# Holding VectorE's background work (block differences, weight sums, third modulation vector) at its place in the text's order

## The chip, the cores and the metric

The kernel runs on one core of a Trainium2 chip. A core has TensorE (PE, with its weight loads listed as PEld), VectorE (DVE), ScalarE (ACT), GpSimd (POOL) and SyncE (SP, which here only issues DMAs); each works through an instruction stream of its own, and they meet at semaphores. The metric is the device time of one execution in microseconds, as the median of several runs. The profile is one further execution, recorded by the hardware profiler.

## The reference

One decoder layer over a sequence of 1024 tokens of width 1024. A conditioning vector gives shift, scale and gate; the normalised, modulated input goes through one wide projection; two gated linear recurrences (HGRN2 with 8 heads, GLA with 4) run on parts of it; both results are projected, merged under sigmoid gates, projected once more, multiplied by the gate vector and added to the input.

```python
c_act = jax.nn.silu(c)
mod = c_act @ ada_w[l] + ada_b[l]
shift, scale, gate = jnp.split(mod, 3, axis=-1)
h = rms_norm(x, norm_w[l]) * (1.0 + scale[:, None, :]) + shift[:, None, :]
proj = h @ w_in[l]
hq, hf, hi, hz, gq, gk, gv, gz, ga, mg = jnp.split(proj, IN_OFFSETS, axis=-1)
y_h = hgrn2_branch(hq, hf, hi, hz, lb_all[l], hgrn_norm_w[l])
y_g = gla_branch(gq, gk, gv, gz, ga, gla_alpha_w[l], gla_alpha_b[l], gla_norm_w[l])
u_h = y_h @ w_branch[l, 0]
u_g = y_g @ w_branch[l, 1]
mg = jax.nn.sigmoid(mg.reshape(B, T, N_BRANCH, D_MODEL))
merged = mg[:, :, 0] * u_h + mg[:, :, 1] * u_g
x = x + gate[:, None, :] * (merged @ w_out[l])
return rms_norm(x, final_norm_w)
```

## The kernel before

All arithmetic is float32. A product of two float32 matrices is made of three TensorE products of rounded parts: `split` (lines 187 to 196) writes the rounded part `hi` on ACT (L192) and the rest `lo` on DVE (L195).

**The main stream.** After the input has been normalised and transposed, a list of jobs (`J`, class `Stream`, from line 770) computes the columns of the projection: `Feat` (128 columns, matmuls at L454), `Vblk` (256 columns, L513 to L515) and `Vblk2` (512 columns, L556 to L558). A job's `run` yields after every few matmuls; one yield is one *unit*. A `Feat` has 8 units of 6 matmuls, a `Vblk` 16, a `Vblk2` 32, the first job 24. Weights are loaded up to two jobs ahead and split up to one job ahead (`ahead`).

**What is woven in.** After each unit `weave` hands time to two tracks. The side track holds the attention heads (`attention`, from line 570): bursts of small DVE operations, each followed by small TensorE products that need them (scores at L596, L628, L683 to L694; states and outputs at L742, L761, L763), with yields between the bursts. The back track holds work that has no user before the last stages:

- `factors` (L1125): for both halves of the rows it loads four 128 x 1024 blocks of h from DRAM (L1133), waits 6 units, and makes four differences on DVE (L1136), each stored by a DMA from POOL's queue (L1137). Eight differences in all.
- `weight_sums` (L1153), sixteen blocks: two loads of 512 KB (L1159, SP's queue), 6 units, then four sums of 128 x 512 on DVE in two pairs 1.5 units apart (L1165 and L1166; L1168 and L1169), then four stores from POOL's queue (L1171).
- `gate_side` (L956): the third modulation vector. Eight loads of 512 KB (L962), eight DVE operations that multiply by a scalar and accumulate in `gacc` (L964, L966), four TensorE products that sum over partitions (L974, L975). It starts once `prepare`, which holds the two others, has ended.

**The last stages** (from line 1342, matmuls at L1313) compute the gates' columns and the branch products with seven products per block instead of eight; they read the stored differences and sums. The output projection (L1083 to L1085) ends the kernel.

**Memory.** All large tiles come from 46 slots of 4 KB per partition (`Slots`), handed out first freed, first used. Who gets a slot waits until its last reader is through. A background block is begun only when 12 slots are free.

**What sets the order.** The Python text says in which order instructions are written down. The framework then orders each engine's stream itself, at compile time: an instruction whose inputs it takes to be ready early can be issued ahead of instructions that stand before it in the text. Only a first stretch (lines 155 to 323) is fixed by hand. `tc.keep_in_program_order(i)` adds one edge: `i` is issued behind the instruction that was written down last before it on the same engine. It is an edge of issue order, without a wait, and it binds `i` alone: later instructions may still pass it, and if its predecessor was itself issued early, `i` may be early too.

The lines that the change touches stand in `gate_side`, `factors` and `weight_sums`.

Of the kernel before, what the change touches and what calls it, by code (L numbers as in the profile page):

```python
# [13 lines left out]
ALU = mybir.AluOpType  # L14
# [68 lines left out]
def hybrid_trunk_kernel(  # L83
# [6 lines left out]
    nc = tc.nc  # L90
# [17 lines left out]
    def mtile():  # L108
        cnt[0] += 1
        return ps_m.tile([P, 512], F32, tag="m", name=f"pm{cnt[0]}")  # L110
# [48 lines left out]
    cs = cp.tile([P, KT], F32, name="cs")  # L159
# [796 lines left out]
    def gate_side():  # L956

        gacc, gbias = S.get([D]), S.get([D])
        nc.sync.dma_start(gbias[0:1, :], ada_b[0:1, 2 * D:3 * D])
        for k in range(KT):  # L960
            b = S.get([D])
            nc.sync.dma_start(b, ada_w[0, k * P:(k + 1) * P, 2 * D:3 * D])  # L962
            if k == 0:
                nc.vector.tensor_scalar_mul(gacc, b, cs[:, 0:1])  # L964
            else:
                nc.vector.scalar_tensor_tensor(gacc, b, cs[:, k:k + 1], gacc, ALU.mult, ALU.add)  # L966
            S.free(b)
            yield 1
        yield 3
        gate_b[0] = S.get([D])  # L970
        for half in range(2):
            sl = slice(half * 512, half * 512 + 512)
            pg = mtile()
            nc.tensor.matmul(pg, ones, gacc[:, sl], start=True, stop=False)  # L974
            nc.tensor.matmul(pg, ones[0:1, :], gbias[0:1, sl], start=False, stop=True)  # L975
            nc.scalar.copy(gate_b[0][:, sl], pg)
        S.free(gacc, gbias)
# [50 lines left out]
    def hgrn_v(h):  # L1028
        def done(v):
            h_state[("v", h // 4)] = v  # L1030
            if h == 0:
                stream.back.append([gate_side(), 4])
        J.append(Vblk2(C_HI + h * P, done, lambda: start_side(hgrn_attention(h), 4)))
# [77 lines left out]
    def part_of(acts, kh, half, kk):  # L1111
        return acts[half][kh * 2 + kk]
# [10 lines left out]
    f_x = new_factors(h_d, "fx")  # L1123

    def factors(acts, f):  # L1125
        sub = nc.vector.tensor_sub
        for kk in range(2):
            while len(S.free_list) < 12:
                yield 1
            y = {}  # L1130
            for b in ("12", "11", "22", "21"):
                y[b] = S.get([T])
                nc.sync.dma_start(y[b], part_of(acts, int(b[0]) - 1, int(b[1]) - 1, kk))  # L1133
            yield 6
            for p, dst, a, b in ((5, "11", "12", "11"), (7, "12", "12", "22"), (6, "22", "22", "11"), (4, "21", "21", "22")):
                sub(y[dst], y[a], y[b])  # L1136
                nc.gpsimd.dma_start(f[p][kk], y[dst])  # L1137
                if p == 7:
                    S.free(y["12"])
                elif p == 6:  # L1140
                    S.free(y["11"])
                yield 1.5
            S.free(y["22"], y["21"])
# [9 lines left out]
    def weight_sums(b, i):  # L1153
        src = sources[b][i]
        while len(S.free_list) < 12:
            yield 1
        x1, x2 = S.get([4, 2, P]), S.get([4, 2, P])
        for kh, x in enumerate((x1, x2)):
            nc.sync.dma_start(x.rearrange("p k a f -> p k (a f)"),  # L1159
                              src[kh * 512:(kh + 1) * 512, :].rearrange("(k p) f -> p k f", p=P))  # L1160
        yield 6
        s1, s2 = S.get([2, 4, P]), S.get([2, 4, P])
        parts = {5: s1[:, 0], 6: s1[:, 1], 3: s2[:, 0], 7: s2[:, 1]}
        add = nc.vector.tensor_add
        add(parts[7], x1[:, :, 0], x1[:, :, 1])  # L1165
        add(parts[5], x1[:, :, 1], x2[:, :, 1])  # L1166
        yield 1.5
        add(parts[6], parts[7], x2[:, :, 1])  # L1168
        add(parts[3], parts[6], x2[:, :, 0])  # L1169
        for p, q in SUMS.items():  # L1170
            nc.gpsimd.dma_start(w_sums[b][i // 2][q][:, i % 2 * 512:i % 2 * 512 + 512],  # L1171
                                parts[p].rearrange("p k f -> p (k f)"))
        S.free(x1, x2, s1, s2)
        yield 3

    def prepare():
        yield from factors(h_d, f_x)
        for b in range(4):
            for i in range(4):
                yield from weight_sums(b, i)  # L1180
# [291 lines left out]
    for b in (2, 3):  # L1472
        for p, i, z in ((3, 3, "11"), (6, 1, "21"), (6, 3, "12"), (7, 2, "22")):
            after(b - 1, p, i, lambda b=b, z=z: load_quad(b, z))
            if b == 3:
                p, i = {(3, 3): (7, 2), (6, 1): (7, 3), (6, 3): (4, 2), (7, 2): (4, 3)}[p, i]
# [64 lines left out]
```

## Time and profile before

| | us |
|---|---|
| median of 3 runs | 1251.0 |
| lowest and highest of the runs | 1249.09, 1251.11 |
| the profiled execution's own time | 1252.38 |
| its span, first to last instruction | 1250.7 |
| mean granted TensorE clock | 0.99 of full speed |

The span is 1.7 us shorter than the profiled execution's own time, which in turn is 1.4 us above the median. The views that are used: the page (busy time by engine), the table of waits (which engine's instruction sat idle until which other instruction ended), the timeline (start, duration, engine, line, tiles, shapes; in brackets the engine's idle time before the row and what ended it), groups of instructions by line, and busy time by window. Background work on DVE runs from 234 to 269 us (L1136), 296 to 607 us (L1165 to L1169) and 636 to 656 us (L964, L966).

### The profile page before, as it was taken

Reading aid. Unit: us, or ns where it says so; the run is one execution under the profiler, and the core shown is the slowest. Engines: PE = TensorE matmul, PEld = TensorE weight load, DVE = VectorE, ACT = ScalarE, POOL = GpSimd, SP = SyncE. Lnnn points to the kernel's source line nnn. Section 1 sums busy time; section 2 is a strip of 40 time slices with the busy share of each in tenths; the row PEclk is TensorE's granted clock in tenths of the full one; section 3 lists DMA queues with packets and bytes.
Section 4 is the critical chain, followed back from the end, with each engine's and each line's share of the span. In section 5 each row is a group of like instructions: output and inputs, shape, how many; then the busy total and the mean of one; then the engine's idle time right before and its main releaser. Section 6 shows DMA issues by size and latency. Waiting matters only on the chain.

```text
span 1250.7 us, 20782 instructions
## 1 busy us (share of the span) xinstructions
PE 1205.7 (96%) x8603; PEld 999.9 (80%) x8603; DVE 765.2 (61%) x1219; ACT 530.4 (42%) x784; POOL 132.4 (11%) x216
## 2 busy tenths in 40 slices
PE   4799999999999999999999999999999999998997
PEld 3676899989798888788887878877888888787786
DVE  5746425494857556777873365695422668979443
ACT  4467713343334344243332323456643644454222
POOL 5510000201211021021110101011110000000000
PEclk9899999999999999999999999999999999999999
DMA  8832100653644167255251212154546556235202
GB/s 269 278 115 86 52 18 18 217 188 102 203 143 144 63 208 254 92 179 174 96 177 45 60 41 68 38 183 169 173 163 225 179 171 201 83 100 170 118 34 101
DMA packets 126928, 168.82 MB, mean 135 GB/s; under 512 B 7019, under 2 KB 97185, under 8 KB 126834
## 3 DMA queue, kind: packets, MB, share of 16 engines
q1 hardware_dynamic: 115234, 129.53, 33.5%
q0 software_dynamic: 11552, 37.97, 7.8%
q8 instruction: 67, 1.10, 0.4%
q14 instruction: 27, 0.22, 0.1%
q10 hardware_dynamic: 48, 0.01, 0.0%
HBM read 125.53 MB, written 41.94 MB: 134 GB/s over the span
## 4 chain that ended last, share of the span: by engine, by line
PE 59%; issue 24%; DVE 8%; DMA 3%; POOL 2%; ACT 2%; SPq 1%; POOLq 0%; DVEq 0%; ACTq 0%
PE pd L454 13%; PE pd L1313 11%; PE sc_ps L1313 5%; PE pm L1313 5%; PE pd L556 2%; PE pd L557 2%; PE pd L558 2%; DVE scT L250 1%; PE pm L761 1%; PE pm L742 1%; PE pm L763 1%; PE pd L1083 1%; PE pd L1084 1%; PE pd L1085 1%; DVE b L195 1%
## 5 line engine op out<-in xcount | busy, mean ns | idle before, releaser
L454 PE MATMUL pd<-b,b 128*128 128x512 f32 x1632 | 386.3, 393 | 0.0
L454 PEld LDWEIGHTS pd<-b,b 128*128 128x128 f32 x1632 | 302.4, 188 | 64.0 <-issue 0.5
L1313 PE MATMUL pd<-b,b 128*128 128x512 f32 x720 | 175.7, 395 | 2.5 <-DVE b L866 1.5
L1313 PEld LDWEIGHTS pd<-b,b 128*128 128x128 f32 x720 | 134.7, 189 | 35.4 <-DVE b L866 1.9
L195 DVE TENSOR_TENSOR b<-b,b 128x1024 fp32r<-128x1024 f32 (+1 forms) x95 | 101.8, 1082 | 74.7 <-ACT b L192 34.8
L192 ACT CAST b<-b 128x1024 fp32r<-128x1024 f32 (+1 forms) x95 | 84.6, 904 | 104.0 <-DVE b L1169 14.7
L1256 DVE TENSOR_TENSOR b<-b,b 128x1024 fp32r<-128x1024 f32 x56 | 68.3, 1224 | 68.5 <-ACT b L1255 46.6
L1255 ACT CAST b<-b 128x1024 fp32r<-128x1024 f32 x56 | 58.5, 1051 | 62.8 <-PE pd L1313 17.2
L1313 PE MATMUL sc_ps<-b,b 128*128 128x512 f32 x324 | 79.0, 391 | 0.3 <-ACT scT L706 0.3
L1313 PE MATMUL pm<-b,b 128*128 128x512 f32 x300 | 72.5, 389 | 3.4 <-DVE b L1256 3.4
L513 PE MATMUL pd<-b,b 128*128 128x256 f32 x256 | 74.2, 290 | 0.0
L515 PE MATMUL pd<-b,b 128*128 128x256 f32 x256 | 72.5, 283 | 0.0
L514 PE MATMUL pd<-b,b 128*128 128x256 f32 x256 | 72.4, 283 | 0.0
L1313 PEld LDWEIGHTS sc_ps<-b,b 128*128 128x128 f32 x324 | 60.4, 188 | 13.6 <-ACT scT L706 0.8
L1313 PEld LDWEIGHTS pm<-b,b 128*128 128x128 f32 x300 | 56.3, 188 | 15.5 <-DVE b L1256 3.8
L1234 DVE TENSOR_TENSOR b<-b,b 128x1024 fp32r<-128x1024 f32 x36 | 45.1, 1263 | 18.1 <-ACT b L1233 10.3
L1171 POOL DMA_DIRECT2D ws<-b x64 | 34.6, 541 | 194.8 <-DVE b L1165 87.1
L556 PE MATMUL pd<-b,b 128*128 128x512 f32 x128 | 52.0, 406 | 0.0
L557 PE MATMUL pd<-b,b 128*128 128x512 f32 x128 | 50.4, 394 | 0.0
L558 PE MATMUL pd<-b,b 128*128 128x512 f32 x128 | 50.4, 394 | 0.0
L648 ACT COPY xb<-b 128x512 f32<-128x512 f32 x48 | 29.5, 620 | 49.3 <-PE sc_ps L628 26.3
L1233 ACT CAST b<-b 128x1024 fp32r<-128x1024 f32 x36 | 37.2, 1049 | 28.9 <-PE pd L1313 10.1
(268 smaller groups left out, 2041.9 us busy)
## 6 DMA issues: line engine op xcount, KB each, us to landing
b<-in_w_in_dram SPq DMA_DIRECT2D x66, 512.0 KB, 4.0
ws<-b POOLq DMA_DIRECT2D x64, 256.0 KB, 3.0
b<-ws SPq DMA_DIRECT2D x32, 512.0 KB, 4.2
b<-in_x_dram SPq DMA_DIRECT2D x16, 512.0 KB, 5.8
b<-in_ada_w_dram SPq DMA_DIRECT2D x32, 256.0 KB, 6.2
b<-in_w_branch_dram SPq DMA_DIRECT2D x16, 512.0 KB, 4.8
b<-h SPq DMA_DIRECT2D x14, 512.0 KB, 4.2
b<-in_w_in_dram SPq DMA_DIRECT2D x24, 256.0 KB, 3.5
```

The source lines that it names most:

```text
L192: i = nc.scalar.copy(hi, src)
L195: (eng or nc.vector).tensor_sub(lo, src, hi.bitcast(F32))
L454: nc.tensor.matmul(ps[0:w, th * 512:(th + 1) * 512], a[:, k, 0:w], b[:, th * 512:(th + 1) * 512], start=(k == 0 and n == 0), stop=(k == KT ...
L513: nc.tensor.matmul(o, lh, hi[:, k % 4, :], start=(k == 0), stop=False)
L514: nc.tensor.matmul(o, lh, lo[:, k % 4, :], start=False, stop=False)
L515: nc.tensor.matmul(o, ll, hi[:, k % 4, :], start=False, stop=(k == KT - 1))
L556: nc.tensor.matmul(o, lh, hi[:, k % 2, :], start=(k == 0), stop=False)
L557: nc.tensor.matmul(o, lh, lo[:, k % 2, :], start=False, stop=False)
L558: nc.tensor.matmul(o, ll, hi[:, k % 2, :], start=False, stop=(k == KT - 1))
L1255: nc.scalar.copy(hi, t)
L1256: nc.vector.tensor_sub(lo, t, hi.bitcast(F32))
L1313: nc.tensor.matmul(o, a[:, sl], c, start=(p in (1, 5) and kt == 0 and n == 0), stop=(kt == 3 and n == 2), skip_group_check=True)
```

## The change

Every DVE operation of `factors` and `weight_sums`, and every accumulating operation of `gate_side`, is passed to `keep_in_program_order`. In `gate_side` the yield moves from behind the operation to between the load and the operation, and grows from 1 unit to 3. No arithmetic, shape, load, store or engine is changed.

```diff
@@ -960,12 +960,13 @@
         for k in range(KT):
             b = S.get([D])
             nc.sync.dma_start(b, ada_w[0, k * P:(k + 1) * P, 2 * D:3 * D])
+            yield 3
             if k == 0:
-                nc.vector.tensor_scalar_mul(gacc, b, cs[:, 0:1])
+                i = nc.vector.tensor_scalar_mul(gacc, b, cs[:, 0:1])
             else:
-                nc.vector.scalar_tensor_tensor(gacc, b, cs[:, k:k + 1], gacc, ALU.mult, ALU.add)
+                i = nc.vector.scalar_tensor_tensor(gacc, b, cs[:, k:k + 1], gacc, ALU.mult, ALU.add)
+            tc.keep_in_program_order(i)
             S.free(b)
-            yield 1
         yield 3
         gate_b[0] = S.get([D])
         for half in range(2):
@@ -1123,7 +1124,8 @@
     f_x = new_factors(h_d, "fx")
 
     def factors(acts, f):
-        sub = nc.vector.tensor_sub
+        def sub(*ops):
+            tc.keep_in_program_order(nc.vector.tensor_sub(*ops))
         for kk in range(2):
             while len(S.free_list) < 12:
                 yield 1
@@ -1161,7 +1163,8 @@
         yield 6
         s1, s2 = S.get([2, 4, P]), S.get([2, 4, P])
         parts = {5: s1[:, 0], 6: s1[:, 1], 3: s2[:, 0], 7: s2[:, 1]}
-        add = nc.vector.tensor_add
+        def add(*ops):
+            tc.keep_in_program_order(nc.vector.tensor_add(*ops))
         add(parts[7], x1[:, :, 0], x1[:, :, 1])
         add(parts[5], x1[:, :, 1], x2[:, :, 1])
         yield 1.5
```

## The prediction

> **What bounds the kernel now.** I began with the page, to see which engine there is to be fed, and then cut out the stretch in which the background work runs (225 to 660 us).
>
> ```profile
> span 1250.7 us, 20782 instructions
> PE 1205.7 (96%) x8603; PEld 999.9 (80%) x8603; DVE 765.2 (61%) x1219; ACT 530.4 (42%) x784; POOL 132.4 (11%) x216
> ...
> 225.00:660.00 435.00, 430.45 (x3862) 367.56 (x3860) 298.44 (x530) 169.27 (x251) 70.24 (x103) 1.00 0.50 162
> ```
>
> The columns of the window are its length, then the busy time of PE, PEld, DVE, ACT and POOL with the number of instructions, then the granted TensorE clock, the DMA share and GB/s. TensorE is busy 430.45 of 435 us at full clock, VectorE 298.44. So TensorE sets the end, and all that any order of VectorE's work can give in this stretch is 435.00 - 430.45 = 4.55 us. The change adds and removes no arithmetic; it can only move TensorE's waits. Those are in the table of waits of the same stretch (total, how often, longest):
>
> ```profile
> PE sc_ps L628 <- DVE tot L631: 1.4, 1, 1.4
> PE sc_ps L683 <- DVE blk L672: 1.4, 1, 1.4
> PE sc_ps L596 <- DVE xb L592: 0.9, 1, 0.9
> PE pm L742 <- ACT b L721: 0.4, 1, 0.4
> PE sc_ps L628 <- DVE blk L611: 0.2, 1, 0.2
> ```
>
> Five waits, 1.4 + 1.4 + 0.9 + 0.4 + 0.2 = 4.3 us: nearly all of the 4.55. Each ends on a score product, or on a product behind the scores. The question for each is whether a background operation stood on VectorE ahead of the instruction that TensorE waited for.
>
> **The change part by part.** First the differences. In the timeline of VectorE ahead of the wait at L683:
>
> ```profile
> 258.65 1.23 DVE L1136 TENSOR_TENSOR b<-b,b 128x1024 f32<-128x1024 f32 x1 [0.40 <-DMA b<-h]
> ...
> 261.23 1.23 DVE L1136 TENSOR_TENSOR b<-b,b 128x1024 f32<-128x1024 f32 x1
> 262.38 0.95 DVE L633 TENSOR_TENSOR b<-b,tot 128x768 f32<-128x768 f32 x1
> ...
> 265.22 1.22 DVE L1136 TENSOR_TENSOR b<-b,b 128x1024 f32<-128x1024 f32 x1
> ...
> 266.86 0.69 DVE L656 TENSOR_TENSOR b<-b,tot 128x512 f32<-128x512 f32 x1 [0.28 <-ACT xb L648]
> 267.47 0.18 DVE L672 COPY_PREDICATED blk<-mask,sc_ps 128x32 f32<-128x32 int32 x1
> ```
>
> Three differences, one of them after an idle 0.40 us for its load, run inside an attention burst, ahead of L633; a fourth follows inside the same burst. L633 is therefore late by up to 262.38 - 258.65 + 0.40 = 4.1 us (one difference lies in the rows left out), and L672, on which L683 waits, ends behind it. The wait of 1.4 us is smaller than the delay, so the whole of it goes if these four leave the burst: **-1.4 us**.
>
> The other wait of 1.4 us is at L628, and weight sums stand ahead of it:
>
> ```profile
> 317.33 0.69 DVE L1165 TENSOR_TENSOR b<-b 128x512 f32<-128x512 f32 x1 [1.71 <-DMA b<-in_w_in_dram]
> 321.33 0.69 DVE L1166 TENSOR_TENSOR b<-b,b 128x512 f32<-128x512 f32 x1 [3.31 <-DMA yg<-b]
> ...
> 322.66 0.69 DVE L1169 TENSOR_TENSOR b<-b,b 128x512 f32<-128x512 f32 x1
> 323.27 1.22 DVE L915 COPY b<-pd 128x1024 f32<-128x1024 f32 x1
> 324.41 0.68 DVE L623 TENSOR_TENSOR xb<-b,tot 128x512 f32<-128x512 f32 x1
> ...
> 328.41 0.37 DVE L631 TENSOR_TENSOR tot<-tot 128x64 f32<-128x64 f32 x1
> ```
>
> VectorE stands still for 1.71 and 3.31 us at the head of its queue, for a load and for the store of another tile whose slot the sum is to use, and everything behind it, the burst from L623 on included, stands too. 323.27 - 315.62 (317.33 less the idle 1.71) = 7.65 us pass before the burst goes on. The wait of 1.4 us goes with it: **-1.4 us**. The two small ones:
>
> ```profile
> 530.05 0.69 DVE L1165 TENSOR_TENSOR b<-b 128x512 f32<-128x512 f32 x1 [2.42 <-PE pd L454]
> ...
> 531.50 0.69 DVE L1169 TENSOR_TENSOR b<-b,b 128x512 f32<-128x512 f32 x1
> ...
> 533.24 0.68 DVE L656 TENSOR_TENSOR b<-b,tot 128x512 f32<-128x512 f32 x1
> ...
> 534.45 0.29 DVE L698 COPY_PREDICATED blk<-mask,sc_ps 128x128 f32<-128x128 int32 x1
> ...
> 560.91 0.69 DVE L1166 TENSOR_TENSOR b<-b,b 128x512 f32<-128x512 f32 x1 [0.19 <-DMA ws<-b]
> ```
>
> At 530 three sums delay L656 and L698, behind which ACT copies the scores and then L721, on which TensorE waits 0.4 us at L742. At 561 one sum (0.69 and an idle 0.19) stands in the burst that ends with L611 and the wait of 0.2 us: together **-0.6 us**. The fifth wait is not the background's:
>
> ```profile
> 504.90 0.69 DVE L1166 TENSOR_TENSOR b<-b,b 128x512 f32<-128x512 f32 x1
> 506.33 0.81 DVE L991 TENSOR_SCALAR b<-b,oml,lb 128x1024 f32<-128x1024 f32 x1 [0.74 <-ACT b L989]
> ...
> 510.98 1.24 DVE L195 TENSOR_TENSOR b<-b,b 128x1024 fp32r<-128x1024 f32 x1
> ...
> 735.60 1.31 PE L596 MATMUL sc_ps<-xb,b 128*32 128x80 f32 x64 [0.88 <-DVE xb L592]
> ```
>
> Between the last sum and the burst (from L991) VectorE idles 0.74 us for ACT, so the sum delays nothing; what stands in the burst is a split of 1.24 us (L195), which the change does not touch. The last row is TensorE's at 735.60, where no sum is left: the same line waits 0.88 us there again. It stays: **0**.
>
> What is added: nothing but order. How far the operations move shows at 504.90 and 530.05. The text has L1165 directly ahead of L1166 in each block, and the L1166 at 504.90 is, counted block by block, the partner of the L1165 at 530.05. It ran 25 us ahead of its place. Held, it no longer reaches the head of the queue before its load is there: the load stands 6 units ahead in the text. The amount that moves:
>
> ```profile
> L1166 DVE TENSOR_TENSOR b<-b,b 128x512 f32<-128x512 f32 x16 | 12.7, 792 | 18.6 <-DMA b<-in_w_branch_dram 4.9 <-DMA yg<-b 3.3 <-PE sc_ps L596 3.3
> ...
> L1165 DVE TENSOR_TENSOR b<-b 128x512 f32<-128x512 f32 x16 | 11.0, 690 | 9.4 <-PE pm L761 4.3 <-PE pd L454 2.7 <-DMA b<-in_w_in_dram 1.9
> ...
> L1136 DVE TENSOR_TENSOR b<-b,b 128x1024 f32<-128x1024 f32 x8 | 9.8, 1222 | 3.9 <-DMA b<-h 3.9
> ...
> L589 DVE TENSOR_TENSOR xb<-b,b 128x256 f32<-128x256 f32 x7 | 4.5, 643 | 0.0
> ```
>
> VectorE idles 18.6 + 9.4 + 3.9 = 31.9 us in front of background work; most of that will go, and 4.3 - 0.9 = 3.4 us of it reach TensorE. The price of holding: each pair of sums (2 x 0.69 = 1.38 us) or difference (1.22 us) must now be run at its place, which may be inside a burst, where before it could be done in a pause. The last row counts the bursts' heads in this stretch: seven. Nothing in the trace shows a held operation; the bounds are 0, if every one falls where VectorE has time (it has 435.00 - 298.44 = 136.6 us of it), and 7 x 1.38 = 9.7 us, if one pair delays one score product in every head. I take 0, because the compiler that orders VectorE's stream orders TensorE's too: a score product that it sees late it puts behind more of the main stream. What it does not see is a transfer that lands late, and those are what holding avoids.
>
> The stores (L1137, L1171) leave POOL's queue as late as the operations that they wait for. Behind them in that queue are other stores and the additions at L899 and L1019, none of which feeds TensorE before a head's end; **0**. The loads (L1159 and the weights of later jobs) can wait longer for a slot on SP's queue, since a sum that runs 25 us later frees its slots 25 us later; they are issued up to two jobs ahead. Cover: one job of 8 units is 48 matmuls.
>
> ```profile
> L454 PE MATMUL pd<-b,b 128*128 128x512 f32 x1632 | 386.3, 393 | 0.0
> ...
> ws<-b POOLq DMA_DIRECT2D x64, 256.0 KB, 3.0
> ...
> L974 PE MATMUL pm<-b,ones x4: 591/592/697, 657.5 to 660.0; 128*128 128x512 f32 x4
> ```
>
> 48 x 386.3 / 1632 = 11.4 us a job. In the text, adds come before the split that reuses their slot, and the split up to 5 units (7.1 us) before its job; a split costs 1.05 + 1.24 us, a store 3.0 us to landing. So even at text pace no split is late; 0, with the loss as a rival below.
>
> The third modulation vector: its eight operations ask for 16 units more (8 x 3 instead of 8 x 1), that is 16 x 1.42 = 23 us later for its end, and `gacc`, `gbias` and one load tile keep their slots so much longer. Its four products and their partners are moved with it and cost TensorE the same. No wait of TensorE is tied to it in the table above; **0**, and if the slots run short, a load or split of one job is put off by 2 units of its 8.
>
> Sum: -1.4 - 1.4 - 0.6 = **-3.4 us**. The profiled execution would take 1252.4 - 3.4 = 1249.0; it stands 1.4 above the median, so the forecast for the median is 1251.0 - 3.4 = **1247.6 us**.
>
> **The rivals.** (a) *The operation is held in the wrong place.* One mechanism: a pair of sums stands on VectorE between the score product that releases a burst and the operation that the next score product needs, so L628 or L683 waits for 1.38 us more. For it: in all of the four waits above a background operation inside a burst was the cause, and the text puts the back track directly behind each burst. Against it: the compiler moves TensorE's products too. Seven heads at 1.38 us cost 9.7, less 3.4 gained, +6.3: 1257.3 us. It decides from five heads on: 5 x 1.38 - 3.4 = +3.5.
>
> (b) *Slots come back late.* A split waits for a slot until the store of a late sum has landed. For it: ACT's splits already wait on background work. Against it: the lead worked out above. Beyond the lead, a late split costs about one store and one split, 3.0 + 2.3 = 5.3 us, and it takes two of them to matter: 1251.0 - 3.4 + 2 x 5.3 = 1258.2 us.
>
> (c) *Nothing is held in effect, or other work takes the place.* The edge goes to the instruction before it in the text, and where that is itself issued early (the second sum of a pair follows the first, and a split such as the L195 above floats too), the held one is early as well; or splits of 1.24 us fill the gap in the burst. Then the waits return elsewhere: 1251.0 us.
>
> (d) *The burst meets GpSimd.*
>
> ```profile
> 300.00 2.34 DVE L1168 TENSOR_TENSOR b<-b,b 128x512 f32<-128x512 f32 x1
> ...
> 299.38 2.40 POOL L899 TENSOR_TENSOR b<-b,b 128x1024 f32<-128x1024 f32 x1 [1.16 <-ACT b L893]
> ```
>
> A sum that mostly takes 0.69 took 2.34 us while POOL added two tiles, 1.65 more; the mean of L1166, 792 against 690 ns, tells of one more such hit (16 x 0.10 = 1.6 us). If the sums leave these places and operations of a burst are hit instead, two hits cost 3.3 us on the path: 1251.0 - 3.4 + 3.3 = 1250.9 us. [...]
>
> **How the numbers follow.** 0.2% is 2.5 us, about what a measurement of this kernel can tell from no change. Forecast (1247.6) 0.45; (a) 0.20; (b) 0.08; (c) 0.17; (d) 0.10. Faster comes from the forecast alone, 0.45; same from (c) and (d), 0.27; slower from (a) and (b), 0.28. The range: below the forecast by as much as the one long wait outside the stretch (3.4 us at L1313, which a new order of slots could move) and a little, to 1243.5; above, to 1255.5, which takes in four of seven heads of (a) and more (1251.0 - 3.4 + 4 x 1.38 = 1253.1) and leaves out its end. The forecast's own range is 1245 to 1249.
>
> **What would show it.** In the profile after: L1136 and L1165 to L1169 start some 25 us later, L1165 ahead of its L1166, with next to no idle time before them; the waits at L683 (266 us) and L628 (327 us) are gone; the wait at L596 is still there; L974 starts near 680 us. It is wrong if TensorE's busy time in 225 to 660 us does not rise above 433 of 435, if new waits for L631 or L672 of over 1 us appear behind a held sum (a), or if splits wait for stores and TensorE for splits (b).

## The result, and the profile after

The changed kernel takes 1255.78 us (median of six runs, 1251.76 to 1256.49), the kernel before 1249.97 in the same set (six runs, 1246.07 to 1251.11): 1.0047 of before, 95% interval [1.0025, 1.0069]. Forecast was 1247.6, in a range up to 1255.5; the change is 5.8 us slower instead of 3.4 us faster. In the changed kernel the differences are at L1128 (before L1136), the sums at L1167 (before L1165 to L1169), and the last stages' matmuls at L1316 (before L1313).

The page after, its span and its busy times:

```profile
span 1254.8 us, 20778 instructions
PE 1210.5 (96%) x8603; PEld 1003.4 (80%) x8603; DVE 765.5 (61%) x1219; ACT 531.0 (42%) x784; POOL 133.1 (11%) x216
```

VectorE's work is the same (765.5 against 765.2 us). TensorE does the same 8603 products and is busy 4.8 us longer, so part of the loss is not idle time at all. What the change set out to do it did; the groups by line after, of VectorE from 225 to 700 us:

```profile
L1167 DVE TENSOR_TENSOR b<-b,b 128x512 f32<-128x512 f32 x48 | 32.7, 693 | 1.0 <-DMA b<-in_w_in_dram 0.5 <-PE pm L763 0.4
...
L1167 DVE TENSOR_TENSOR b<-b 128x512 f32<-128x512 f32 x16 | 11.1, 694 | 4.7 <-PE pm L761 4.3 <-PE pm L763 0.4
...
L1128 DVE TENSOR_TENSOR b<-b,b 128x1024 f32<-128x1024 f32 x8 | 9.8, 1220 | 0.1
```

The idle time in front of the background work fell from 31.9 to 1.0 + 4.7 + 0.1 = 5.8 us. But the waits of TensorE from 225 to 660 us read:

```profile
PE sc_ps L628 <- DVE tot L631: 3.8, 1, 3.8
PE sc_ps L596 <- DVE xb L592: 0.9, 1, 0.9
PE pm L742 <- ACT b L721: 0.7, 1, 0.7
```

The two waits of 1.4 us and the one of 0.2 us are gone, as forecast. So is the one of 0.4 us, which lay at 538.86 us: the wait of 0.7 us at the same line lies at 417.79 and is new (more of it under "Two instructions"). A second new wait, of 3.8 us, is not the old one at 327 us but lies at 255 us; VectorE's timeline there:

```profile
242.94 2.48 DVE L1128 TENSOR_TENSOR b<-b,b 128x1024 f32<-128x1024 f32 x2
245.33 1.22 DVE L915 COPY b<-pd 128x1024 f32<-128x1024 f32 x1
247.89 0.69 DVE L623 TENSOR_TENSOR xb<-b,tot 128x512 f32<-128x512 f32 x1 [1.34 <-PE sc_ps L596]
254.09 1.23 DVE L195 TENSOR_TENSOR b<-b,b 128x1024 fp32r<-128x1024 f32 x1 [5.50 <-DMA fx<-b]
255.23 0.42 DVE L603 TENSOR_TENSOR blk<-sc_ps,eye 128x256 f32<-128x256 f32 x1
...
258.60 0.37 DVE L631 TENSOR_TENSOR tot<-tot 128x64 f32<-128x64 f32 x1
```

In the middle of a burst, between L623 and L603, stands a split (L195) of a later job's weights, and it idles 5.50 us until a store of a difference (`fx<-b`) has landed: it is to write into the slot that this store still reads. The two differences ahead of it ran at 242.94, where before they ran at 234.01. Their stores, in POOL's timeline, and the row of the DMA view from 243 to 256 us (KB, then median us to landing):

```profile
244.45 0.54 POOL L1139 DMA_DIRECT2D fx<-b  x1 [0.40 <-DVE b L1128]
245.71 0.53 POOL L1139 DMA_DIRECT2D fx<-b  x1 [0.72 <-DVE b L1128]
```

```profile
fx<-b POOLq DMA_DIRECT2D x2, 512.0 KB, 7.9
```

The row's 7.9 us is the median of the two stores; the second took the longer, 8.2 us, and landed at 245.71 + 8.19 = 253.90. The split starts at 254.09. Behind it wait L603 to L631, and behind L631 TensorE. The clock follows; the windows (length, busy PE, PEld, DVE, ACT, POOL, then clock, DMA share, GB/s), first before, then after:

```profile
256.00:264.00 8.00, 8.00 (x97) 6.43 (x96) 7.60 (x14) 1.24 (x2) 1.60 (x3) 1.00 0.53 169
830.00:838.00 8.00, 6.53 (x89) 5.18 (x88) 7.83 (x18) 2.74 (x6) 0.00 (x0) 1.00 0.30 105
```

```profile
258.00:266.00 8.00, 6.99 (x84) 5.69 (x85) 7.27 (x21) 3.52 (x5) 0.53 (x1) 0.79 0.29 65
834.00:842.00 8.00, 8.00 (x90) 6.22 (x89) 6.22 (x17) 2.87 (x4) 0.00 (x0) 0.79 0.20 68
```

A mean of 0.79 over 8 us is (1 - 0.79) x 8 = 1.7 us of clock lost, which is 3.4 us at half rate (the mean is 0.50 from 260.59 to 264.00 us). The profile after has this twice where the one before does not, behind the wait of 3.8 us and behind one in the stage after, whose rows in the waits from 660 to 860 us are, before and after:

```profile
PE pd L1313 <- DVE b L866: 1.5, 1, 1.5
```

```profile
PE pd L1316 <- DVE b L866: 2.4, 1, 2.4
```

The account: waits from 225 to 660 us 5.4 against 4.3, +1.1; halved clock behind, +1.7; the wait for L866, +0.9; halved clock behind that, +1.7: together +5.4. This is an account of two single executions, and it has to be set against their own difference. Their spans differ by 1254.8 - 1250.7 = 4.1 us, but the one after is 2.0 us ahead before any of this begins (its first matmul at L454 starts at 126.1 us, before at 128.1), so it loses 6.1 us from there on. Behind a wait of 3.3 to 3.4 us near 1143 us, which both have, the clock is also halved for 6.8 us after and for 3.4 us before, 1.7 us more; with it the terms come to 7.1, and 1.0 us the other way is not accounted for. Only the first two terms, 2.8 us together, come from 225 to 660 us, where the background work of the change runs. Whether the others belong to the change these two profiles can't tell.

### The profile page after: what moved, and what is told of

Read it like the earlier page. It is cut to its first block, busy times and chain, and to the rows that moved or that the text cites. A ratio compares the mean times of both kernels' runs of the same rounds, so it can differ in the third digit from the quotient of the medians.

```text
span 1254.8 us, 20778 instructions
## 1 busy us (share of the span) xinstructions
PE 1210.5 (96%) x8603; PEld 1003.4 (80%) x8603; DVE 765.5 (61%) x1219; ACT 531.0 (42%) x784; POOL 133.1 (11%) x216
## 4 chain that ended last, share of the span: by engine, by line
PE 63%; issue 16%; DVE 6%; POOL 2%; DMA 2%; ACT 2%; POOLq 0%; DVEq 0%; ACTq 0%
PE pd L454 19%; PE pd L1316 9%; PE sc_ps L1316 5%; PE pm L1316 4%; PE pd L556 2%; PE pd L557 2%; PE pd L558 2%; PE pd L515 2%; PE pd L514 2%; PE pd L513 2%; PE pm L761 2%; PE pm L742 1%; PE pm L763 1%; PE pd L1084 1%; PE pd L1086 1%
## 5 line engine op out<-in xcount | busy, mean ns | idle before, releaser
L454 PE MATMUL pd<-b,b 128*128 128x512 f32 x1632 | 389.9, 396 | 0.0
L454 PEld LDWEIGHTS pd<-b,b 128*128 128x128 f32 x1632 | 304.6, 189 | 66.0 <-issue 1.2
L1316 PE MATMUL pd<-b,b 128*128 128x512 f32 x720 | 178.1, 399 | 3.5 <-DVE b L866 2.4
L1316 PEld LDWEIGHTS pd<-b,b 128*128 128x128 f32 x720 | 136.3, 192 | 36.9 <-DVE b L866 2.8
L195 DVE TENSOR_TENSOR b<-b,b 128x1024 fp32r<-128x1024 f32 (+1 forms) x95 | 102.9, 1096 | 78.6 <-ACT b L192 39.3
L1316 PE MATMUL sc_ps<-b,b 128*128 128x512 f32 x324 | 79.0, 391 | 0.3 <-ACT scT L706 0.3
L1316 PE MATMUL pm<-b,b 128*128 128x512 f32 x300 | 73.0, 391 | 3.3 <-DVE b L1259 3.3
L1316 PEld LDWEIGHTS sc_ps<-b,b 128*128 128x128 f32 x324 | 60.4, 188 | 13.6 <-ACT scT L706 0.7
L1316 PEld LDWEIGHTS pm<-b,b 128*128 128x128 f32 x300 | 56.7, 189 | 15.6 <-DVE b L1259 3.7
```

What stands on the lines that cost most here:

```text
L195: (eng or nc.vector).tensor_sub(lo, src, hi.bitcast(F32))
L454: nc.tensor.matmul(ps[0:w, th * 512:(th + 1) * 512], a[:, k, 0:w], b[:, th * 512:(th + 1) * 512], start=(k == 0 and n == 0), stop=(k == KT ...
L1316: nc.tensor.matmul(o, a[:, sl], c, start=(p in (1, 5) and kt == 0 and n == 0), stop=(kt == 3 and n == 2), skip_group_check=True)
```

## Experiments

Three theories went into them. A, late slots: the split in VectorE's queue that waits for the store of a held difference. B: held operations cost time inside the bursts, wherever they stand. C: the later place of the third modulation vector changes what follows. Each ratio is against runs of the kernel before on the same chip; the medians of before in the three sets are 1250.35, 1249.07 and 1250.19 us.

### One part alone

Three kernels make one part of the change in the kernel before, a fourth all parts but the first.

```diff
 differences alone:             +  def sub(*ops): tc.keep_in_program_order(nc.vector.tensor_sub(*ops))
 sums alone:                    +  def add(*ops): tc.keep_in_program_order(nc.vector.tensor_add(*ops))
 third vector alone:            +  yield 3  ...  +  tc.keep_in_program_order(i)  ...  -  yield 1
 all but the differences:       the second and the third
```

> Only the eight differences are held; sums and the third modulation vector as before. Theory A (late slots): VectorE again stands still for some 5 us in front of a split that waits for a store of a difference, TensorE waits 3 to 4 us at L628 near 255 us, the granted clock is halved for 3.4 us behind it (1.7 us lost), and the wait of 1.4 us at L683 near 266 us is gone: about +4 us, 1.003 of before. Theory B (pairs of sums inside the bursts): the differences are few, within 1 us of before. Theory C (the third modulation vector's move): no difference.

> Only the sixteen blocks of sums are held. Theory A: no long wait near 255 us; the wait of 1.4 us at L628 near 327 us goes, a wait of some 0.7 us at L742 may come: about -2 us, 0.998 of before. Theory B: the whole loss of 5 to 6 us is here, 1.0045. Theory C: no difference.

> Only the third modulation vector is held and spread (3 units instead of 1 each). Theory A: same time as before within 1 us. Theory B: the same. Theory C: the later slots after 700 us change, TensorE waits some 2.4 us for L866 near 830 us with a halved clock behind it: about +2.6 us, 1.002.

> The whole change without the differences: sums and third modulation vector held. Theory A: about -2 us, 0.998 of before. Theory B: +5 us, 1.004. Theory C: between -2 and +2.6.

| held | median us | ratio to before | 95% |
|---|---|---|---|
| differences | 1255.26 | 1.0039 | [1.0022, 1.0056] |
| sums | 1249.19 | 0.9988 | [0.9975, 1.0000] |
| third vector | 1250.94 | 1.0008 | [0.9993, 1.0023] |
| all but differences | 1249.20 | 0.9987 | [0.9973, 1.0000] |

The eight differences carry the loss; the sums, eight times as many operations, cost nothing and may gain a little (the interval ends at 1.0000). B is out as a general cause. The trace of the differences alone has the same place: the split, its idle time and TensorE's wait (VectorE's timeline, then TensorE's waits from 225 to 660 us):

```profile
254.31 1.22 DVE L195 TENSOR_TENSOR b<-b,b 128x1024 fp32r<-128x1024 f32 x1 [5.38 <-DMA fx<-b]
```

```profile
PE sc_ps L628 <- DVE tot L631: 4.3, 2, 3.6
```

The third vector alone is worth nothing that these runs can tell; its profile has the wait for L866 of 2.3 us without a halved clock behind it (1.00 from 826 to 834 us), so C is not borne out by the time.

### Another slot for the split

If it is the slot, the loss must go when the tiles of a group give their slots back later, so that the split is handed another one.

```diff
                 sub(y[dst], y[a], y[b])
                 nc.gpsimd.dma_start(f[p][kk], y[dst])
-                if p == 7:
-                    S.free(y["12"])
-                elif p == 6:
-                    S.free(y["11"])
                 yield 1.5
-            S.free(y["22"], y["21"])
+            yield 12
+            S.free(*y.values())
```

This was put into the whole change, into the change without the third vector, into the kernel before, and into the kernel with the differences alone.

> The whole change, but the four tiles of a group of differences give their slots back 12 units after the last store instead of right behind each, so the next split is handed another slot. Theory A (the split in VectorE's queue waits for the store of a held difference): the idle 5.5 us ahead of the split near 254 us and TensorE's wait of 3.8 us at L628 are gone, no halved clock near 260 us, and the waits of 1.4 us at L683 and L628 of before do not return: 0.998 to 0.999 of before. Theory B (held operations inside the bursts cost it): the loss stays, 1.004.

> Differences and sums held, slots given back later as in the run before, third modulation vector as in the kernel before. Theory A: the gains of both kinds without the loss, 0.997 to 0.999. Theory B: 1.004.

> The kernel before with only the later return of the slots; nothing is held. It tells whether the later return is worth something by itself. Theory A: within 0.1% of before, since no split waits there for a store at a cost to TensorE. If it is itself as fast as the two runs above, those do not show what they are meant to.

> Only the differences held, with the later return of the slots: the run of the differences alone, less the one suspected wait. Theory A: from 1.004 to between 0.998 and 1.000, no wait over 1 us at L628 near 255 us. Theory B: 1.004 still.

| with slots given back later | median us | ratio to before | 95% |
|---|---|---|---|
| the change | 1249.08 | 0.9998 | [0.9986, 1.0010] |
| the change without the third vector | 1258.17 | 1.0079 | [1.0057, 1.0102] |
| the kernel before | 1256.73 | 1.0060 | [1.0040, 1.0079] |
| differences alone | 1252.86 | 1.0029 | [1.0012, 1.0046] |

Where the wait had been, theory A's expectation held in all three kernels with held differences: no wait at L628 is left in any of their tables from 225 to 660 us. The change's, complete:

```profile
PE sc_ps L596 <- DVE xb L592: 0.9, 1, 0.9
PE pm L761 <- DVE b L748: 0.4, 1, 0.4
```

But the times missed in all four, of the change by little (0.9998 against 0.998 to 0.999), of the others by far, and the control tells why. The 12 units put off all later background work, and other waits came. In the control (waits from 225 to 660 us) they are:

```profile
PE pm L742 <- ACT b L721: 2.2, 3, 1.5
PE sc_ps L628 <- DVE blk L611: 1.8, 1, 1.8
PE sc_ps L628 <- DVE tot L631: 1.8, 1, 1.8
```

So these four agree that the wait at 255 us hangs on the slot; they do not show what it costs. The worst of them has its wait elsewhere. In the change without the third vector, ACT's part of a split waits 8.00 us for the store of a held sum, and behind it on ACT stand L989 and L990, which the burst needs. The vector's operations, not held, float into the same burst (ACT's timeline; VectorE's, the last of them before L592; then TensorE's waits from 660 to 860 us):

```profile
723.38 2.00 ACT L192 CAST b<-b 128x1024 fp32r<-128x1024 f32 x2 [8.00 <-DMA ws<-b]
725.28 1.02 ACT L989 ACTIVATE b<-pd 128x1024 f32<-128x1024 f32 x1
```

```profile
725.61 1.28 DVE L966 SCALAR_TENSOR_TENSOR b<-b,cs,b 128x1024 f32<-128x1024 f32 x1
...
727.53 1.28 DVE L966 SCALAR_TENSOR_TENSOR b<-b,cs,b 128x1024 f32<-128x1024 f32 x1
...
732.49 1.27 DVE L966 SCALAR_TENSOR_TENSOR b<-b,cs,b 128x1024 f32<-128x1024 f32 x1
733.68 0.63 DVE L592 TENSOR_TENSOR xb<-xb,b 128x256 f32<-128x256 f32 x1
```

```profile
PE sc_ps L596 <- DVE xb L592: 7.6, 1, 7.6
```

The three operations are 3.8 us of VectorE's time; the split's 8.00 us on ACT are the mechanism of theory A once more, with a sum's store and on another queue. In the change with the same later return, where the vector is held and spread, this wait is 0.9 us. Holding and spreading it is worth nothing in the order of slots of the kernel before and much in this one; how much of that is the three operations and how much the slot that the split is handed, no run separates.

### Two instructions

The cleaner test leaves the order of the text and of the slots alone. Of the eight differences only the first two of the first group end so close ahead of the split; the mark is taken from these two, or set on them alone (the condition is then `kk == 0 and p in (5, 7)`). The other six differences, all sums and the third vector stay held in the first kernel; the change has 80 marks (8 differences, 64 sums, 8 of the vector), not the 16 that its expectation counts.

```diff
         def sub(*ops):
-            tc.keep_in_program_order(nc.vector.tensor_sub(*ops))
+            i = nc.vector.tensor_sub(*ops)
+            if kk or p not in (5, 7):
+                tc.keep_in_program_order(i)
```

> The whole change, but the first two differences of the first group are not held (14 of the 16 marks on differences and sums' blocks and all of the vector's stay as they are; the slots and the text are those of the change). Theory A: these two are the whole loss, since the store of the second is what the split waits for. They go back to 234 us, their stores too, and the idle 5.5 us, TensorE's 3.8 us at L628 and the halved clock behind are gone: 0.998 of before. Theory B: the loss is spread over the held operations, 1.004.

> Only differences held, without the first two of the first group. Theory A: from 1.004 (all eight held) to 0.998 to 1.000. Theory B: 1.003 to 1.004.

> The kernel before with only the first two differences of the first group held: two marks. Theory A: the split waits for the second's store as in the change, TensorE waits over 2 us at L628 near 255 us: 1.003 to 1.005. Theory B: within 0.1% of before.

> Sums held and the differences but the first two; third modulation vector as before. If theory A is right this is the change without its loss and without the part that is worth nothing: 0.997 to 0.999. Theory B: 1.004.

| held | median us | ratio to before | 95% |
|---|---|---|---|
| the change, but those two differences | 1247.43 | 0.9980 | [0.9967, 0.9993] |
| the other six differences alone | 1248.58 | 0.9985 | [0.9972, 0.9998] |
| those two alone | 1256.63 | 1.0053 | [1.0040, 1.0067] |
| sums and the other six | 1248.88 | 0.9995 | [0.9982, 1.0008] |

Two marks in the kernel before cost 6.4 us (1256.63 - 1250.19), as much as the whole change; the change without the two is 2.8 us faster than the kernel before (1250.19 - 1247.43) and has the lowest ratio of all versions tried, though the intervals of several overlap. In its trace (VectorE, POOL, TensorE's waits from 225 to 660 us, and that window's busy times):

```profile
232.77 2.48 DVE L1128 TENSOR_TENSOR b<-b,b 128x1024 f32<-128x1024 f32 x2 [0.64 <-DMA b<-h]
...
245.05 1.23 DVE L195 TENSOR_TENSOR b<-b,b 128x1024 fp32r<-128x1024 f32 x1 [2.01 <-ACT b L192]
```

```profile
235.56 0.53 POOL L1141 DMA_DIRECT2D fx<-b  x1 [0.69 <-DVE b L1128]
```

```profile
PE sc_ps L596 <- DVE xb L592: 0.9, 1, 0.9
PE pm L742 <- ACT b L721: 0.7, 1, 0.7
```

```profile
225.00:660.00 435.00, 433.39 (x3871) 370.65 (x3870) 294.11 (x527) 168.84 (x250) 70.56 (x103) 1.00 0.49 160
```

The store leaves 10 us earlier (235.56 against 245.71), the split no longer waits for it, and TensorE's waits are 1.6 us instead of 4.3. With those two alone held, the split idles again, 4.56 us, and L628 waits 3.8 us. The view names no releaser; that it is the second store is inferred. The stores of differences start there from 243.3 us on and take up to 8.6 us to landing, and the split starts at 252.97:

```profile
252.97 1.23 DVE L195 TENSOR_TENSOR b<-b,b 128x1024 fp32r<-128x1024 f32 x1 [4.56 <-issue]
```

```profile
PE sc_ps L628 <- DVE tot L631: 5.4, 2, 3.8
```

The granted clock of every single run of these kernels is on record (to 0.001, or 1.25 us of the span), and it says how much of this is clock. The clock lost, (1 - clock) x span, is on average 15.0 us in the six runs of the change, 14.7 with the differences alone and 15.5 with those two alone. It is 11.8 to 12.2 us in the three sets of the kernel before, 11.9 in the change without the two and 11.6 with the other six alone (13.4 with the third vector alone, 13.2 with sums and the other six). So of the 4.9 to 6.4 us that the three slow kernels lose, some 3 to 3.6 are clock, on average over their runs and not only in a profile.

The new wait of 0.7 us at L742 stayed. It is in all five profiles with held sums and the slots as they were (411 to 418 us) and in no other. It has the same pattern on a smaller scale; in the profile of the change (ACT, VectorE, TensorE):

```profile
407.35 1.05 ACT L192 CAST b<-b 128x1024 fp32r<-128x1024 f32 x1 [1.68 <-DVE b L1167]
```

```profile
408.43 1.23 DVE L195 TENSOR_TENSOR b<-b,b 128x1024 fp32r<-128x1024 f32 x1 [1.11 <-ACT b L192]
```

```profile
417.79 1.56 PE L742 MATMUL pm<-b,b 128*128 128x256 f32 x6 [0.68 <-ACT b L721]
```

A split waits for a held sum, first on ACT and so on VectorE, and the burst behind it (L656, L657, L698) is late. This is the price of holding the sums.

Two of these four miss their expectation by a little: the two alone with 1.0053, where 1.003 to 1.005 was expected, and the last kernel with 0.9995, where 0.997 to 0.999 was expected. The last kernel's profile has the wait of 2.4 us for L866 with a halved clock behind it (0.79 from 827 to 835 us), the profile of the fastest has 1.5 us. That wait is 2.3 or 2.4 us in the change, with the third vector alone, with the two differences alone and here, and 1.4 or 1.5 us in all other profiles. The third vector's place does not decide it: of these four profiles two hold the vector and two do not, and three others hold it with 1.5 us. What stands in that burst is an addition on POOL; the operation of VectorE that it meets is another one (VectorE and POOL after, then VectorE before):

```profile
817.97 3.09 DVE L598 TENSOR_TENSOR b<-b,b 128x256 f32<-128x256 f32 x1
```

```profile
818.15 2.40 POOL L1020 TENSOR_TENSOR b<-b,b 128x1024 f32<-128x1024 f32 x1
```

```profile
818.73 2.22 DVE L592 TENSOR_TENSOR xb<-xb,b 128x256 f32<-128x256 f32 x1
```

In the median of their lines the two take 0.63 (L598 after) and 0.64 us (L592 before). Here they take 3.09 and 2.22, and each ends 0.5 us after the addition that runs beside it (before: L1019, 2.72 us from 817.71). The difference, 0.87, is as large as that of the two waits, 0.9 us. Why it is the one or the other stays open: the addition starts 0.18 us behind L598 after and 0.19 us before. So nothing ties these 0.9 us, and the clock behind them, to the change.

## Why the prediction was wrong

**TensorE sets the end, and only its waits can move: right**, but not complete. Of the 5.4 us in the account 3.4 are clock lost behind waits, which the bound of 4.55 us of idle time did not hold. The prediction's own sign was TensorE's busy time from 225 to 660 us, which was to rise above 433 us: it fell from 430.45 to 429.54 in the change, and it is 433.39 without the two marks.

**The four waits of 3.4 us belong to the background work: right.** All four went (L683, both at L628, L742 at 539 us), and the one at L596 stayed. With all held but the two differences, the waits from 225 to 660 us fall from 4.3 to 1.6, by 2.7 us and not by 3.4, because the new one of 0.7 us came; the time falls by 2.8.

**Held operations at their place cost nothing: nearly right, at a price of 0.7 us.** The sums, held alone, came out at 0.9988 [0.9975, 1.0000]. In the change no score product waits for a held pair of sums, as rival (a) had it, to which I gave 0.20. But one wait behind a held sum did appear, the 0.7 us at L742, and not by way of (a): a split that waits for the sum holds up the burst.

**"So even at text pace no split is late; 0": this step failed.** It asked whether a split is late for the job that uses it, and none was. It did not ask what stands behind the split on VectorE. The split is not held, so it floats ahead of its place in the text, into a burst; and there it waits for a slot whose last reader is a store of an operation that is held. How far ahead can be estimated: it stands at the head of VectorE's queue when L623 ends, at 248.6 us, and by the order of the splits it belongs to the `Vblk` whose matmuls start at 276.33; at most 7.1 us before its job, as the prediction counts, its place is not before 269, some 20 us later. What was late was not the split's own product but the burst in the same queue. Rival (b) named the late store, with 0.08, but put the price at a split's own lead and asked for two events; one event at the head of VectorE's queue was enough, at 6.4 us [1.0040, 1.0067] when made alone.

**Of the stores I wrote that nothing behind them on POOL's queue feeds TensorE: true, and not the question.** The reader of the slot counts, and it stood on VectorE's queue. Nor did 3.0 us to landing, the median of the sums' stores of 256 KB, fit: this one, of 512 KB and together with others, took 8.2. The trace of before had that size to show, since there the stores of differences took up to 8.9 us.

**The third modulation vector: 0, right.** 1.0008 [0.9993, 1.0023]; L975, the products, moved to 682.6 us as forecast (near 680).

**The forecast's size** would have been near without the two differences: 3.4 us forecast, 2.8 measured, with an interval of 0.9 to 4.1 us.

## What to carry to other kernels

When an operation is moved later, follow its slot: who is the next owner, on which engine's queue does that owner stand now, and what stands behind it there. Holding some operations and not the ones that take over their memory can turn a harmless early start of the latter into a wait at the head of a queue (5.50 us in the change). What holding gained here, 0.1 to 0.2%, is near the edge of what these runs can tell. Test it instruction by instruction, since two marks of eighty carried the whole loss.

## What the runs showed of the hardware

A wait of TensorE cost more than its length here. Behind the waits of 3.8 us (the change, and the two differences alone) the mean granted clock was 0.79 over 8 us, behind 3.6 us (differences alone) 0.66 over 10 us, and behind 7.6 us 0.77 over 15 us: halved for 3.4 to 6.8 us, 1.7 to 3.4 us lost. Behind 2.4 us it was halved too in the three profiles that have that wait (0.79 over 8 us in each), and behind 2.3 us, with the third vector alone, it was not (1.00 over 8 us).

The waits of 2.4 and 2.3 us lie differently to the steps in which the clock changed. In the profile after, the halved stretches later than 70 us start at 260.6, 687.2, 834.0, 1148.0 and 1250.5 us, whole multiples of 3.413 us apart (125, 43, 92 and 30); before they start at 661.4, 1146.1 and 1245.1 us (142 and 29). The 2.35 us from 830.51 lie nearly all (2.25) in one step, and the next step is at half clock. The 2.33 us of the third vector alone, from 825.68 to 828.01, lie across a border, by my estimate at 826.66 (93 steps before its halved stretch at 1144.1). Of TensorE's time 0.98 us are idle in the stretch ahead of it and 1.35 in the one behind, and the clock is at 1.00 throughout (the steps of the change, then those of the third vector alone):

```profile
830.60:834.00 3.40, 1.14 (x5) 0.97 (x6) 3.40 (x5) 1.20 (x3) 0.00 (x0) 1.00 0.43 172
834.00:837.40 3.40, 3.40 (x10) 2.61 (x9) 3.40 (x9) 0.17 (x1) 0.00 (x0) 0.50 0.44 154
```

```profile
823.25:826.66 3.41, 2.43 (x57) 1.70 (x46) 3.41 (x4) 3.01 (x6) 0.00 (x0) 1.00 0.93 291
826.66:830.07 3.41, 2.06 (x9) 1.71 (x10) 3.41 (x7) 0.56 (x2) 0.00 (x0) 1.00 0.23 93
830.07:833.48 3.41, 3.41 (x17) 2.71 (x15) 3.38 (x8) 1.08 (x2) 0.00 (x0) 1.00 0.45 154
```

Idle time in a step does not decide it alone. The wait of 3.77 us near 255 us in the profile after lies across a border too, with 3.41 - 1.48 = 1.93 us on one side and 3.42 - 1.58 = 1.84 on the other. The step behind the first is at full clock, the one behind the second is halved:

```profile
253.76:257.17 3.41, 1.48 (x7) 0.90 (x5) 3.08 (x6) 0.00 (x0) 0.00 (x0) 1.00 0.39 141
257.17:260.59 3.42, 1.58 (x67) 1.46 (x68) 3.35 (x9) 0.62 (x1) 0.00 (x0) 1.00 0.00 0
260.59:264.00 3.41, 3.41 (x9) 2.63 (x8) 3.38 (x10) 0.91 (x2) 0.53 (x1) 0.50 0.14 16
```

In the profiles before and after, from 75 us on, all four steps at full clock with 2.2 us or more of idle time were followed by a halved one (2.55 us before; 2.25, 2.84 and 3.25 after). Of three with 1.8 to 2.0 us two were (1.97 before, 1.84 after) and one was not (1.93 after). After a step at full clock with 1.5 us or less it happened once in each, behind the step in which the products for the third vector run (before: L974 and L975, 658.0 to 661.4 us; after: 683.8 to 687.2), though the profile has TensorE busy throughout (3.41 of 3.41 us). The borders of the two profiles lie 1.4 us off each other (from 260.58 after to 661.37 before it is 117 steps and 1.4 us). That what a wait of two to four microseconds costs in clock is in part chance is my estimate from these numbers.
